# Two layers of a hybrid decoder: the norms of the rows one tile behind their sums, and three weight pieces split ahead of the last expert pair

## The chip, the cores and the metric

One core of a Trainium2 chip runs the whole program in one launch. The metric is the device time of one execution in microseconds (us), median of several; lower is better. The core's engines run side by side, each with its own queue of instructions that it works off in order: TensorE (PE) multiplies matrices, VectorE (DVE) and GpSimd (POOL) work elementwise, ScalarE (ACT) applies functions and copies, SyncE (SP) issues most DMAs. SBUF is the on-chip memory, PSUM holds what PE writes.

## What is computed

A decoder trunk of two layers over 512 tokens of width 1024. Each layer has a token mixer and a mixture of 32 experts, both behind a norm that is modulated by vectors computed from `c`; a last norm ends the program. Cut to what matters here:

```
for layer in range(2):
    h = rmsnorm(x, norm_mix_g) * (1 + sc_mix) + sh_mix
    x = x + g_mix * token_mixer(h, w_in, ..., w_out)      # begins with h @ w_in
    h = rmsnorm(x, norm_ffn_g) * (1 + sc_ffn) + sh_ffn
    x = x + g_ffn * moe(h, ...)                            # 4 groups x 8 experts, 2 per token
return rmsnorm(x, final_norm_g)                            # x * rsqrt(mean(x*x) + 1e-6) * g
# moe: y += (silu(t @ w_gate) * (t @ w_up) * weight of the token) @ w_down, per expert
```

## The kernel before

The tokens stand in four row tiles of 128 (i = 0 to 3). The 32 experts are worked off as 16 pairs, n = 0 to 15, one pair in a matmul of 128 rows. The loop over the pairs (L1816 to L1836) issues `gate_up(n)`, then `down(n-1)`, so that a pair's silu on ACT and DVE (L770 to L774, tiles `sg`, `sge`) runs beside other matmuls. `down(n)` transposes the pair's hidden rows on PE (L1754), copies them to SBUF on ACT (`hT`, L1756), multiplies by w_down (L1767) and scales by the gate vector on DVE (`y`, L1773).

The rows of the first 12 pairs go through memory. Those of pairs 12 to 15 are put to their tokens by matmuls: ACT and POOL (or DVE) divide `y` into a rounded part `yh` (L1776) and its remainder `yl` (L1777), and `combine(n)` multiplies both by a 0/1 matrix (L1806, L1807) and adds the sum to `x` on DVE (L1808), eight times for a pair. For pair 15, `combine` goes tile by tile, and behind each half of a tile it sums its squares on ACT (`junk`, L1446); in layer 0, POOL besides scales the half for the next norm (tile `z`, L1450).

After that stand the norms. `route_norm(i)` adds the two half sums on DVE (`ssum`, L1597) and calls `rstd`: DVE `m` (L569), ACT logarithm and exponential (L570, L571), DVE `nt` and `y` (L574, L578), all of one element per row. In layer 0, `next_hT` then makes the next mixer's input for each tile: DVE `z` (L662), eight PE transposes (L672) with copies into `hhi` (ACT) and `hlo` (DVE, L676). In the last layer, `final` writes each tile into a new tile `fy` (L1913) and sends it (L1914); the gain `fg` is loaded on ACT's queue (L1909).

A weight piece of the mixer is likewise used as a rounded part and its remainder. A piece is 512 rows by up to 512 columns, loaded to a tile `w` and split in two halves by `split`: ACT writes the rounded part (L240), then `lo_engine`, which is DVE unless it is set, the remainder (L241). `splitter` returns the function `get` that makes splits when they are first asked for; `in_open` makes that function for a layer's pieces of `w_in`, and `next_hT` asks for the first halves between the tiles. Their matmuls are L740 (hi by hi), L741 and L742.

The loads of all weights go out on SP in one order (L216), each when a slot of SBUF is free; `rows`, the next norm's vectors spread over all partitions, is loaded by two DMAs on ACT's queue (L531), which `next_open` issues in the code behind `down(15)`.

The order on each engine is set by a scheduler from the order of the code; where `pin` or `keep_in_program_order` is set, the instruction keeps its place in the code's order.

Of the kernel before, what the change touches and what calls it, by code (L numbers as in the profile page):

```python
# [10 lines left out]
F32 = mybir.dt.float32  # L11
# [124 lines left out]
class Kernel:  # L136
# [366 lines left out]
    def ada_fin(self, l, v):  # L503
        V, T, acc, c = self.V, self.T, self.acc, self.c
        if (l, v) == (0, 0):
            vec = self.const([P, 2, NK], F32, "vec")
            p = self.pb()
            rows = self.ident.rearrange("p (v j r) -> p j v r", v=2, j=2)[:, :, :, 0]
            for j in range(2):
                for k in range(NK):  # L510
                    T.matmul(p[j * 64:j * 64 + 64, 2 * k:2 * k + 2], acc.rearrange("p (q k) -> p k q", k=NK)[:, k, :],
                             rows[:, j], start=True, stop=True)
            part = self.split
            self.split = lambda w, n, los=[V, V, self.G]: self.pinned(part, los.pop(0), w, n)
            self.in_open(0)
            self.split = part
            V.tensor_tensor(vec, p[:, 0:2 * NK].rearrange("p (k v) -> p v k", v=2),
                            c["bada"].rearrange("p (v k) -> p v k", v=2), op=OP.add)
            V.scalar_tensor_tensor(vec[:, 1], vec[:, 1], 1.0, c["gmix"], op0=OP.add, op1=OP.mult)
            self.vec[(0, 0)], self.vec[(0, 1)] = vec[:, 0], vec[:, 1]  # L520
            return
# [80 lines left out]
            self.next_hT(l)  # L602

    def in_open(self, l):
        self.hhi = [self.u([P, 4, L], F32R, "hhi") for _ in range(2)]
        self.hlo = [self.u([P, 4, L], F32R, "hlo") for _ in range(2)]
        self.get = self.splitter([st for st in self.mseq[l] if st[0] == "in"] + self.oseq[l])
        if l == 0:
            self.get(("in", l, 0, 0), 0)

    def first_hT(self):
        V, S, G, T = self.V, self.S, self.G, self.T
# [39 lines left out]

    def next_hT(self, l):
        V, S, G, T = self.V, self.S, self.G, self.T
        self.mixer_slots()
        self.in_open(l)
        self.mixer_open(l)
        for i in range(NT):
            self.route_norm(i)
            h = self.h[i]  # L660
            self.tc.keep_in_program_order(
                V.scalar_tensor_tensor(h, h, self.r[i], self.rows[:, 0], op0=OP.mult, op1=OP.add))  # L662
            if i < 3:
                self.pin = True
                self.get(("in", l, 0, 0), 0, i + 1)
                self.pin = False
            self.nc.scalar.dma_start(self.xd[i * P:(i + 1) * P, :], self.xt[i])
            hh = h.rearrange("p (q k) -> p q k", k=NK)
            for g in range(2):
# [944 lines left out]
    def moe(self, l):  # L1614
# [184 lines left out]
        def combine(n):  # L1799
            for a in range(8):  # L1800
# [8 lines left out]
                if n == NE // 2 - 1:  # L1809
                    self.route_half(i, half)  # L1810
                    if half and self.h:
                        self.route_scale(i, half)

        self.reserve, got = 3, None
        self.pump()
        for n in range(NE // 2):  # L1816
            gate_up(n)
            if n == 0:
                self.overflow(l, *over)
# [18 lines left out]
            self.next_open(l + 1)  # L1838
        else:
            self.h, self.ssq, self.r = {}, {}, {}  # L1840
        combine(NE // 2 - 1)

    def overflow(self, l, cnti, ov):
# [17 lines left out]
        with self.tc.If(any_ > 0):  # L1861
            nc.scalar.dma_start(self.ovd, ov.rearrange("p i e -> p (i e)"))
            nc.scalar.dma_start(self.ovc, cnti[:, 0:NE])
            with self.tc.For_i(0, NE, 1) as e:
                nc.scalar.dma_start(ce, self.ovc[:, ds(e, 1)])
                here = nc.values_load(ce[0:1, 0:1], min_val=0, max_val=2 * L)
                with self.tc.If(here > 0):
# [7 lines left out]
                    for i in range(NT):  # L1875
# [21 lines left out]
                        for h in range(2):  # L1897
                            cs = slice(h * 512, h * 512 + 512)
                            p = pd
                            for f in range(2):  # L1900
# [2 lines left out]
                            V.scalar_tensor_tensor(self.xt[i][:, cs], y, wv[:, i:i + 1], self.xt[i][:, cs],  # L1903
                                                   op0=OP.mult, op1=OP.add)

    def final(self):
        V, S = self.V, self.S
        g = self.t4([P, D], F32, "fg")
        self.nc.scalar.dma_start(g, self.dap("final_norm_g", 0, [[0, P], [1, D]]))  # L1909
        for i in range(NT):  # L1910
            self.route_norm(i)
            y = self.t4([P, D], F32, "fy")
            V.scalar_tensor_tensor(y, self.xt[i], self.r[i], g, op0=OP.mult, op1=OP.mult)  # L1913
            self.nc.sync.dma_start(bass.AP(tensor=self.out.tensor, offset=self.out.offset + i * P * D,  # L1914
                                           ap=[[D, P], [1, D]]), y)


    def merge(self, main, sides):
# [69 lines left out]
```

## Time and profile before

| | |
|---|---|
| median of 3 runs | 1335.87 us (1334.55 to 1336.6) |
| profiled execution | 1337.54 us |
| its span (first to last instruction) | 1335.8 us |
| mean granted TensorE clock | 0.95 of full speed |
| PE, DVE, ACT, POOL busy | 87%, 54%, 30%, 26% of the span |
| second layer's first matmul of `w_in` starts | 694.22 us |
| first final row starts | 1325.57 us |

All times in the rows below are microseconds from the span's start in the one profiled execution. A timeline row reads: start, duration, engine (with a q where a DMA is issued), line, operation, what is written from what, shape, count; in brackets the idle time of that engine before it and what ended it. A row with a count above 1 covers several instructions in succession, and its duration is from the first's start to the last's end.

### The profile page before, as it was taken

Reading aid. Unit: us, or ns where it says so; the run is one execution under the profiler, and the core shown is the slowest. Engines: PE = TensorE matmul, PEld = TensorE weight load, DVE = VectorE, ACT = ScalarE, POOL = GpSimd, SP = SyncE. Lnnn points to the kernel's source line nnn. Section 1 sums busy time; section 2 is a strip of 40 time slices with the busy share of each in tenths; the row PEclk is TensorE's granted clock in tenths of the full one; section 3 lists DMA queues with packets and bytes.
Section 4 is the critical chain, followed back from the end, with each engine's and each line's share of the span. In section 5 each row is a group of like instructions: output and inputs, shape, how many; then the busy total and the mean of one; then the engine's idle time right before and its main releaser. Section 6 shows DMA issues by size and latency. Waiting matters only on the chain. (4 is left out here: it accounts for less than half of the span.)

```text
span 1335.8 us, 16642 instructions
## 1 busy us (share of the span) xinstructions
PE 1164.3 (87%) x5900; PEld 729.9 (55%) x5902; DVE 718.7 (54%) x1576; ACT 401.1 (30%) x1029; POOL 350.7 (26%) x299
## 2 busy tenths in 40 slices
PE   4888899999999988788969998999898999888785
PEld 3666566666774443345347765767576644334432
DVE  3786877876671211123686576787777221112266
ACT  3442422545321211111135332345352121111113
POOL 0252323461242111111033222346133321111100
PEclk9898989999989999997989997989999999999898
DMA  9973256462877999999972221463276899999972
GB/s 377 400 283 116 76 190 248 124 228 63 312 239 281 413 411 403 391 397 403 392 265 77 73 95 36 171 228 116 94 285 209 261 409 412 413 411 411 401 315 79
DMA packets 104861, 350.95 MB, mean 263 GB/s; under 512 B 16875, under 2 KB 27883, under 8 KB 90435
## 3 DMA queue, kind: packets, MB, share of 16 engines
q1 hardware_dynamic: 85936, 313.31, 61.7%
q10 hardware_dynamic: 10738, 22.24, 4.8%
q0 software_dynamic: 8096, 14.24, 3.0%
q8 instruction: 51, 0.84, 0.3%
q14 instruction: 40, 0.32, 0.1%
HBM read 333.35 MB, written 29.48 MB: 272 GB/s over the span
## 5 line engine op out<-in xcount | busy, mean ns | idle before, releaser
L1732 PE MATMUL pa<-w,X 128*64 128x512 f32 x1024 | 259.0, 605 | 41.9 <-DMA w<-w_up 35.2
L1732 PEld LDWEIGHTS pa<-w,X 128*64 128x64 f32 x1024 | 102.7, 138 | 163.5 <-issue 113.9
L1767 PE MATMUL pb<-w,hT 128*64 128x512 f32 x512 | 137.9, 639 | 11.8 <-ACT hT L1756 10.7
L740 PE MATMUL pa<-wp,hhi 128*128 128x512 f32 x320 | 135.1, 426 | 3.7 <-ACT hhi L639 3.6
L741 PE MATMUL pa<-wp,hhi 128*128 128x512 f32 x320 | 130.1, 407 | 0.9 <-DVE wp L241 0.9
L742 PE MATMUL pa<-wp,hlo 128*128 128x512 f32 x320 | 128.3, 403 | 0.8 <-DVE hlo L640 0.8
L1741 DVE TENSOR_SCALAR sg<-pa 128x256 f32<-128x256 f32 x32 | 13.6, 424 | 208.4 <-PE pa L1732 208.4
L241 DVE TENSOR_TENSOR wp<-w,wp 128x1024 fp32r<-128x1024 f32 (+1 forms) x71 | 93.7, 1328 | 38.0 <-ACT wp L240 37.7
L1780 POOL DMA_INDIRECT yd<-y,idx x24 | 24.0, 1001 | 306.9 <-DVE y L1770 265.3
L240 ACT ACTIVATE wp<-w 128x1024 fp32r<-128x1024 f32 (+1 forms) x72 | 72.3, 1014 | 94.6 <-PE pa L742 38.3
L1767 PEld LDWEIGHTS pb<-w,hT 128*64 128x64 f32 x512 | 47.8, 145 | 78.1 <-issue 46.4
L1717 ACT ACTIVATE X<-pa 128x512 f32<-128x512 f32 x56 | 31.9, 598 | 183.1 <-PE pa L1716 164.5
L740 PEld LDWEIGHTS pa<-wp,hhi 128*128 128x128 f32 x320 | 62.1, 195 | 27.8 <-issue 6.5
L1770 DVE TENSOR_TENSOR y<-pb,gbc 128x512 f32<-128x512 f32 x48 | 33.2, 692 | 73.3 <-PE pb L1767 72.5
L770 ACT ACTIVATE sge<-sg 128x256 f32<-128x256 f32 x32 | 13.2, 412 | 197.8 <-DVE sg L1741 184.0
L742 PEld LDWEIGHTS pa<-wp,hlo 128*128 128x128 f32 x320 | 62.2, 195 | 16.8 <-issue 1.7
L741 PEld LDWEIGHTS pa<-wp,hhi 128*128 128x128 f32 x320 | 62.7, 196 | 15.2 <-DVE wp L241 1.9
L919 POOL TENSOR_TENSOR QX<-E,qk 128x1024 f32<-128x1024 f32 x16 | 40.6, 2536 | 96.6 <-ACT E L917 58.8
L1337 PE MATMUL pa<-wp,mhi 128*128 128x512 f32 x128 | 52.7, 411 | 0.7 <-ACT mhi L1310 0.5
L1339 PE MATMUL pa<-wp,mlo 128*128 128x512 f32 x128 | 51.8, 404 | 1.2 <-DVE mlo L1311 1.2
L935 PE MATMUL pb<-QX,E 64*128 64x128 f32 x448 | 43.8, 293 | 9.4 <-DVE hkg L1012 5.3
L1338 PE MATMUL pa<-wp,mhi 128*128 128x512 f32 x128 | 50.9, 398 | 0.0
(350 smaller groups left out, 2184.7 us busy)
## 6 DMA issues: line engine op xcount, KB each, us to landing
w<-w_gate SPq DMA_DIRECT2D x128, 512.0 KB
w<-w_up SPq DMA_DIRECT2D x128, 512.0 KB
w<-w_down SPq DMA_DIRECT2D x64, 1024.0 KB
w<-w_ada SPq DMA_DIRECT2D x48, 1024.0 KB
w<-w_in SPq DMA_DIRECT2D x16, 1024.0 KB
w<-w_in SPq DMA_DIRECT2D x16, 512.0 KB
yd<-Sblk SPq DMA_DIRECT2D x8, 1024.0 KB
w<-w_out SPq DMA_DIRECT2D x8, 1024.0 KB
```

Of the source, the lines that this page charges most:

```text
L240: keep(self.S.activation(hi, w[:, sl, :], AF.Copy))
L241: keep(self.lo_engine.tensor_tensor(lo, w[:, sl, :], hi.bitcast(F32), op=OP.subtract))
L740: T.matmul(acc[i], hh[:, s], wh, start=k == 0, stop=False)
L741: T.matmul(acc[i], hh[:, s], wl, start=False, stop=False)
L742: T.matmul(acc[i], hl[:, s], wh, start=False, stop=k == NK - 1)
L919: G.tensor_tensor(qx, e, qk[i][:, pr, None, :].to_broadcast([P, 8, P]), op=OP.mult)
L935: T.matmul(o, e[r, lv, :], qx[r, lv, :], start=True, stop=True)
L1337: T.matmul(acc, mh[kh][:, kk, s], hi[:, kk % 2, :], start=first, stop=False)
L1338: T.matmul(acc, mh[kh][:, kk, s], lo[:, kk % 2, :], start=False, stop=False)
L1339: T.matmul(acc, ml[kh][:, kk, s], hi[:, kk % 2, :], start=False, stop=last)
L1732: mm = T.matmul(p[j * 64:j * 64 + 64, :], X[h][:, kh * 4 + kk, ep * P + j * 64:ep * P + j * 64 + 64], w[j][:, :, kk], start=kh == 0 and kk ...
L1767: T.matmul(p[j * 64:j * 64 + 64, :], hT[:, f, j * 64:j * 64 + 64], w[j][:, f, cs], start=f == 0, stop=f == 1)
```

## The change

Three edits.

1. `in_open(l)` no longer makes `hhi` and `hlo` (a new `hh_open` does) and always asks for its first pieces. For layer 1 it is called ahead of `gate_up(15)` of layer 0, with `pin` set and POOL as the engine of the remainder. That is three splits: both halves of the first piece of `w_in` and the first half of the second. `next_hT` no longer asks for splits between the tiles. For layer 0 the order is as before.
2. In `combine(15)`, `route_norm(i - 1)` stands behind the second half of tile i, for i = 1 to 3. The last tile's norm stays where it was.
3. In the last layer, the final row of tile i - 1 is formed there too, in place in `x`, without the tile `fy`; `final_open` issues the load of `fg`.

```
 def in_open(self, l):
-    self.hhi = [self.u([P, 4, L], F32R, "hhi") for _ in range(2)]
-    self.hlo = [self.u([P, 4, L], F32R, "hlo") for _ in range(2)]
     self.get = self.splitter([st for st in self.mseq[l] if st[0] == "in"] + self.oseq[l])
-    if l == 0:
-        self.get(("in", l, 0, 0), 0)
+    self.get(("in", l, 0, 0), 0)
+
+def hh_open(self):
+    self.hhi = [self.u([P, 4, L], F32R, "hhi") for _ in range(2)]
+    self.hlo = [self.u([P, 4, L], F32R, "hlo") for _ in range(2)]
...
 def next_hT(self, l):
-    self.mixer_slots()
-    self.in_open(l)
+    self.hh_open()
     self.mixer_open(l)
     for i in range(NT):
-        self.route_norm(i)
+        if i not in self.r:
+            self.route_norm(i)
...
-        if i < 3:
-            self.pin = True
-            self.get(("in", l, 0, 0), 0, i + 1)
-            self.pin = False
...
 def combine(n):
...
                     if half and self.h:
                         self.route_scale(i, half)
+                    if half and i > 0:
+                        self.route_norm(i - 1)
+                        if not self.h:
+                            self.final_tile(i - 1)
...
         for n in range(NE // 2):
+            if n == NE // 2 - 1 and l + 1 < DEPTH:
+                self.mixer_slots()
+                self.pin, self.lo_engine = True, G
+                self.in_open(l + 1)
+                self.pin, self.lo_engine = False, V
             gate_up(n)
...
             self.h, self.ssq, self.r = {}, {}, {}
+            self.final_open()
         combine(NE // 2 - 1)
...
+def final_open(self):
+    self.fg = self.t4([P, D], F32, "fg")
+    self.nc.scalar.dma_start(self.fg, self.dap("final_norm_g", 0, [[0, P], [1, D]]))
+
+def final_tile(self, i):
+    x = self.xt[i]
+    self.V.scalar_tensor_tensor(x, x, self.r[i], self.fg, op0=OP.mult, op1=OP.mult)
+    self.nc.sync.dma_start(bass.AP(tensor=self.out.tensor, offset=self.out.offset + i * P * D,
+                                   ap=[[D, P], [1, D]]), x)
+
 def final(self):
-    V, S = self.V, self.S
-    g = self.t4([P, D], F32, "fg")
-    self.nc.scalar.dma_start(g, self.dap("final_norm_g", 0, [[0, P], [1, D]]))
-    for i in range(NT):
-        self.route_norm(i)
-        y = self.t4([P, D], F32, "fy")
-        V.scalar_tensor_tensor(y, self.xt[i], self.r[i], g, op0=OP.mult, op1=OP.mult)
-        self.nc.sync.dma_start(bass.AP(tensor=self.out.tensor, offset=self.out.offset + i * P * D,
-                                       ap=[[D, P], [1, D]]), y)
+    self.route_norm(NT - 1)
+    self.final_tile(NT - 1)
```

What this does to the order on the engines, at three places. In the names, the first number counts the tiles and the last one the writes; `w_985` and `w_986` are the first two pieces of the next layer's `w_in`.

ACT at the last pair of layer 0, before. The two `yh` at the top belong to pair 13, `sge` to the silu of pair 15, `hT` and the last two `yh` to pair 14.

```order
L1776 ACTIVATE yh_963_4952<-y_966_4959 128x512
L1776 ACTIVATE yh_963_4952<-y_968_4968 128x512
L770 ACTIVATE sge_986_5053<-sg_985_5051 128x256
L1756 ACTIVATE hT_988_5062<-pb_987_5059 128x256
L773 ACTIVATE sge_986_5053<-sge_986_5053 128x256
L531 DMA rows_1015_5151<-vecd_115 128x1024
L774 ACTIVATE sge_986_5053<-sge_986_5053 128x256
L531 DMA rows_1015_5151<-vecd_115 128x1024
L1776 ACTIVATE yh_989_5064<-y_992_5071 128x512
```

The same place on ACT now.

```order
L1774 ACTIVATE yh_963_4952<-y_966_4959 128x512
L1774 ACTIVATE yh_963_4952<-y_968_4968 128x512
L240 ACTIVATE wp_979_5024<-w_985_5033 128x1024
L240 ACTIVATE wp_980_5025<-w_985_5033 128x1024
L240 ACTIVATE wp_981_5026<-w_986_5039 128x1024
L532 DMA rows_1015_5153<-vecd_115 128x1024 x2
L768 ACTIVATE sge_989_5062<-sg_988_5060 128x256
L1754 ACTIVATE hT_991_5071<-pb_990_5068 128x256
L771 ACTIVATE sge_989_5062<-sge_989_5062 128x256
L772 ACTIVATE sge_989_5062<-sge_989_5062 128x256
L1774 ACTIVATE yh_992_5073<-y_995_5080 128x512
```

Three splits and both DMAs of `rows` now stand ahead of the silu of pair 15 and of the `hT` for which PE's `down(14)` waits. In the program, the first of the two DMAs waits for POOL's remainder of `wp_980`, since `rows_1015` is given the place of `w_985` in SBUF, and POOL's remainder is the last that reads it.

DVE at the start of the norms behind the last pair of layer 0, before. The two rows ahead are the last sums into `x`; `z_1016` is the next mixer's input of tiles 0 and 1.

```order
L1808 TENSOR_TENSOR x_518_2749<-pb_1033_5201,x_518_2749 128x512
L1808 TENSOR_TENSOR x_518_2749<-pb_1036_5209,x_518_2749 128x512
L1597 TENSOR_TENSOR ssum_1050_5231<-ssq_1019_5160 128x1
L569 TENSOR_SCALAR m_1051_5233<-ssum_1050_5231 128x1
L574 SCALAR_TENSOR_TENSOR nt_1053_5238<-m_1051_5233,y_1052_5234 128x1
L1597 TENSOR_TENSOR ssum_1056_5259<-ssq_1024_5175 128x1
L578 SCALAR_TENSOR_TENSOR y_1052_5234<-nt_1053_5238,y_1052_5234 128x1
L569 TENSOR_SCALAR m_1057_5261<-ssum_1056_5259 128x1
L662 SCALAR_TENSOR_TENSOR z_1016_5154<-z_1016_5154,y_1052_5234,rows_1015_5151 128x1024
L241 TENSOR_TENSOR wp_1038_5216<-w_983_5047,wp_1038_5216 128x1024
```

The same place on DVE now, from the last sum into `x`; the first `ssum` and `m` stand among the sums.

```order
L1806 TENSOR_TENSOR x_518_2749<-pb_1044_5231,x_518_2749 128x512
L575 SCALAR_TENSOR_TENSOR nt_1031_5195<-m_1029_5190,y_1030_5191 128x1
L579 SCALAR_TENSOR_TENSOR y_1030_5191<-nt_1031_5195,y_1030_5191 128x1
L1595 TENSOR_TENSOR ssum_1037_5213<-ssq_1024_5177 128x1
L570 TENSOR_SCALAR m_1038_5215<-ssum_1037_5213 128x1
L575 SCALAR_TENSOR_TENSOR nt_1040_5220<-m_1038_5215,y_1039_5216 128x1
L1595 TENSOR_TENSOR ssum_1046_5238<-ssq_1033_5202 128x1
L579 SCALAR_TENSOR_TENSOR y_1039_5216<-nt_1040_5220,y_1039_5216 128x1
L570 TENSOR_SCALAR m_1047_5240<-ssum_1046_5238 128x1
L575 SCALAR_TENSOR_TENSOR nt_1049_5245<-m_1047_5240,y_1048_5241 128x1
L579 SCALAR_TENSOR_TENSOR y_1048_5241<-nt_1049_5245,y_1048_5241 128x1
L664 SCALAR_TENSOR_TENSOR z_1016_5156<-z_1016_5156,y_1030_5191,rows_1015_5153 128x1024
```

Between the last sum and the first `z` there stood six small instructions: the norm of tile 0 with `ssum` and `m` of tile 1. Now the rest of the norms of tiles 0 to 2 stands there, with the `ssum` of tile 3, and no remainder of a weight piece follows.

DVE at the end of the last layer, before.

```order
L1808 TENSOR_TENSOR x_1484_7670<-pb_1993_10104,x_1484_7670 128x512
L1597 TENSOR_TENSOR ssum_1996_10112<-ssq_1976_10062 128x1
L569 TENSOR_SCALAR m_1997_10114<-ssum_1996_10112 128x1
L574 SCALAR_TENSOR_TENSOR nt_1999_10119<-m_1997_10114,y_1998_10115 128x1
L1597 TENSOR_TENSOR ssum_2001_10125<-ssq_1981_10075 128x1
L578 SCALAR_TENSOR_TENSOR y_1998_10115<-nt_1999_10119,y_1998_10115 128x1
L569 TENSOR_SCALAR m_2002_10127<-ssum_2001_10125 128x1
L1913 SCALAR_TENSOR_TENSOR fy_2000_10122<-x_1483_7669,y_1998_10115,fg_1995_10110 128x1024
```

And now.

```order
L1595 TENSOR_TENSOR ssum_1986_10086<-ssq_1977_10064 128x1
L1806 TENSOR_TENSOR x_1484_7670<-pb_1993_10105,x_1484_7670 128x512
L570 TENSOR_SCALAR m_1987_10088<-ssum_1986_10086 128x1
L1806 TENSOR_TENSOR x_1484_7670<-pb_1999_10123,x_1484_7670 128x512
L575 SCALAR_TENSOR_TENSOR nt_1989_10093<-m_1987_10088,y_1988_10089 128x1
L1595 TENSOR_TENSOR ssum_1995_10111<-ssq_1982_10077 128x1
L1806 TENSOR_TENSOR x_1484_7670<-pb_2002_10130,x_1484_7670 128x512
L579 SCALAR_TENSOR_TENSOR y_1988_10089<-nt_1989_10093,y_1988_10089 128x1
L570 TENSOR_SCALAR m_1996_10113<-ssum_1995_10111 128x1
L1920 SCALAR_TENSOR_TENSOR x_1483_7669<-x_1483_7669,y_1988_10089,fg_1975_10058 128x1024
```

The first tile's norm stands among the last sums into `x`, and ACT's logarithm for it now stands between the sums of squares and not behind all of them; the first final row follows two small instructions behind the last sum.

## Rows read from the trace of the kernel before

**Rows 1.** The page's first part: busy time of each engine, its share of the span, and its instructions.

```profile
PE 1164.3 (87%) x5900; PEld 729.9 (55%) x5902; DVE 718.7 (54%) x1576; ACT 401.1 (30%) x1029; POOL 350.7 (26%) x299
```

**Rows 2.** The waits of PE over the whole span. Columns: engine, tile and line that waited, for what; total us, times, longest us.

```profile
PE pb L672 <- DVE z L662: 9.4, 2, 8.5
```

**Rows 3.** The timeline of ACT from 655 to 668 us, around the silu of pair 15.

```profile
660.14 0.42 ACT L770 ACTIVATE sge<-sg 128x256 f32<-128x256 f32 x1 [11.47 <-DVE sg L1741]
660.46 0.36 ACT L1756 ACTIVATE hT<-pb 128x256 f32<-128x256 f32 x1
...
664.71 0.33 ACTq L531 DMA_DIRECT2D rows<-vecd  x1
665.16 1.15 ACT L1776 ACTIVATE yh<-y 128x512 fp32r<-128x512 f32 x2 [3.53 <-DMA w<-w_in]
```

**Rows 4.** The timeline of PE from 655 to 672 us: the last transposes ahead of `down(14)`, `down(14)`, and the first matmuls of `combine(14)`.

```profile
659.49 0.50 PE L1754 MATMUL pb<-first,sg 128*128 128x128 f32 x2
660.88 3.65 PE L1767 MATMUL pb<-w,hT 128*64 128x512 f32 x16 [0.89 <-ACT hT L1756]
665.84 0.97 PE L1806 MATMUL pb<-yh,PT 128*128 128x512 f32 x3 [1.30 <-ACT yh L1776]
667.27 0.97 PE L1807 MATMUL pb<-yl,PT 128*128 128x512 f32 x3 [0.46 <-POOL yl L1777]
```

**Rows 5.** The DMA issues of SP in three stretches (640 to 646.5, 646.5 to 650, and 664 to 667 us): pieces of the next layer's `w_in`. A duration is the time that SP stands at the issue.

```profile
645.62 0.38 SPq L216 DMA_DIRECT2D w<-w_in  x1
...
646.89 9.28 SPq L216 DMA_DIRECT2D w<-w_in  x2
...
663.08 1.54 SPq L216 DMA_DIRECT2D w<-w_in  x1
```

**Rows 6.** Busy time of each engine in four stretches. Columns: window, us, busy us of PE, PEld, DVE, ACT and POOL with their instructions, granted clock of PE, DMA share, GB/s.

```profile
654.00:657.00 3.00, 3.00 (x16) 1.06 (x16) 2.70 (x3) 0.00 (x0) 0.00 (x0) 1.00 1.04 394
685.00:686.00 1.00, 0.00 (x0) 0.00 (x0) 1.00 (x2) 0.55 (x1) 1.00 (x2) 0.97 0.73 303
696.00:697.00 1.00, 1.00 (x5) 0.79 (x4) 1.00 (x2) 0.82 (x1) 0.00 (x0) 0.91 1.07 416
1318.00:1322.00 4.00, 3.28 (x13) 1.91 (x11) 4.00 (x8) 2.42 (x7) 0.00 (x0) 1.00 0.01 3
```

**Rows 7.** Prices of a split: all of ACT's rounded parts as a group (busy us, mean ns, idle before), and the one remainder that POOL makes in this kernel, at its start (timeline of POOL, 0 to 40 us).

```profile
L240 ACT ACTIVATE wp<-w 128x1024 fp32r<-128x1024 f32 x64 | 66.9, 1055 | 84.3 <-PE pa L742 38.3 <-DMA w<-w_in 16.3 <-PE pa L727 12.4
...
37.03 2.60 POOL L241 TENSOR_TENSOR wp<-w,wp 128x1024 fp32r<-128x1024 f32 x1 [36.57 <-ACT wp L240]
```

**Rows 8.** The timeline of all engines from 662 to 675 us: `y`, `yh` and `yl` of pairs 14 and 15.

```profile
662.87 0.69 DVE L1773 TENSOR_TENSOR y<-pb,gbc 128x512 f32<-128x512 f32 x1 [1.79 <-PE pb L1767]
...
665.93 1.29 POOL L1777 TENSOR_TENSOR yl<-y,yh 128x512 fp32r<-128x512 f32 x1 [17.66 <-ACT yh L1776]
...
673.91 0.69 DVE L1773 TENSOR_TENSOR y<-pb,gbc 128x512 f32<-128x512 f32 x1 [1.22 <-PE pb L1767]
...
674.64 0.63 ACT L1776 ACTIVATE yh<-y 128x512 fp32r<-128x512 f32 x1 [2.76 <-DVE y L1773]
```

**Rows 9.** The timeline of DVE from 677 to 692 us: the last sums into `x` of layer 0 and the norms.

```profile
677.26 0.69 DVE L1808 TENSOR_TENSOR x<-pb,x 128x512 f32<-128x512 f32 x1 [0.94 <-PE pb L1807]
...
678.47 4.36 DVE L1808 TENSOR_TENSOR x<-pb,x 128x512 f32<-128x512 f32 x7
682.75 0.69 DVE L1597 TENSOR_TENSOR ssum<-ssq 128x1 f32<-128x1 f32 x1
...
684.64 1.24 DVE L574 SCALAR_TENSOR_TENSOR nt<-m,y 128x1 f32<-128x1 f32 x1 [1.01 <-ACT y L571]
685.80 1.30 DVE L1597 TENSOR_TENSOR ssum<-ssq 128x1 f32<-128x1 f32 x1
687.02 1.30 DVE L578 SCALAR_TENSOR_TENSOR y<-nt,y 128x1 f32<-128x1 f32 x1
...
688.40 1.28 DVE L662 SCALAR_TENSOR_TENSOR z<-z,y,rows 128x1024 f32<-128x1024 f32 x1
689.61 1.22 DVE L241 TENSOR_TENSOR wp<-w,wp 128x1024 fp32r<-128x1024 f32 x1
690.74 0.21 DVE L574 SCALAR_TENSOR_TENSOR nt<-m,y 128x1 f32<-128x1 f32 x1
```

**Rows 10.** The timelines of POOL from 676 to 692 us and of PE from 680 to 700 us, the same stretch.

```profile
678.03 10.27 POOL L1450 TENSOR_TENSOR z<-x,rows 128x512 f32<-128x512 f32 x8 [1.36 <-DVE x L1808]
...
680.83 0.40 PE L1807 MATMUL pb<-yl,PT 128*128 128x512 f32 x1
689.75 1.97 PE L672 MATMUL pb<-first,z 128*128 128x128 f32 x8 [8.52 <-DVE z L662]
...
694.22 0.78 PE L740 MATMUL pa<-wp,hhi 128*128 128x512 f32 x1
```

**Rows 11.** The timelines of DVE and of ACT from 1317 to 1334 us, the end of the program, and of ACT's DMA issues from 1314 to 1317 us.

```profile
1318.90 4.36 DVE L1808 TENSOR_TENSOR x<-pb,x 128x512 f32<-128x512 f32 x7
...
1325.57 1.28 DVE L1913 SCALAR_TENSOR_TENSOR fy<-x,y,fg 128x1024 f32<-128x1024 f32 x1
...
1324.61 0.19 ACT L570 ACTIVATE y<-m 128x1 f32<-128x1 f32 x1
...
1315.15 0.35 ACTq L1909 DMA_DIRECT2D fg<-final_norm_g  x1
```

More of the change, by code (lines that the diff above doesn't have):

```diff
@@ L604, in in_open @@
     def in_open(self, l):
+        self.get = self.splitter([st for st in self.mseq[l] if st[0] == "in"] + self.oseq[l])
+        self.get(("in", l, 0, 0), 0)
+    def hh_open(self):
         self.hhi = [self.u([P, 4, L], F32R, "hhi") for _ in range(2)]
         self.hlo = [self.u([P, 4, L], F32R, "hlo") for _ in range(2)]
-        self.get = self.splitter([st for st in self.mseq[l] if st[0] == "in"] + self.oseq[l])
-        if l == 0:
-            self.get(("in", l, 0, 0), 0)
     def first_hT(self):
@@ L654, in next_hT @@
         V, S, G, T = self.V, self.S, self.G, self.T
-        self.mixer_slots()
-        self.in_open(l)
+        self.hh_open()
         self.mixer_open(l)
         for i in range(NT):
-            self.route_norm(i)
+            if i not in self.r:
+                self.route_norm(i)
             h = self.h[i]
```

## The prediction

> **What bounds the kernel now.** I read the busy shares first: PE works 87% of the span and no other engine over 54% [rows 1], so a change elsewhere counts only where PE stands still, or after its last matmul. PE's waits as a whole then show where the norms at the layer's boundary cost something: PE waits 9.4 us for `z`, 8.5 of them at once [rows 2]. The timelines of that place tell what is late. The first sum of pair 15 into `x` starts at 677.26 (call this X) and the first `z` at 688.40, which is X + 11.14 [rows 9]; PE, idle since 681.23, goes on at 689.75 and begins the next layer's first matmul at 694.22 [rows 10]. At the end of the program the first final row starts at 1325.57, after ACT's first logarithm at 1324.61 [rows 11]. The change works on both places. What it puts ahead of them, three splits, lands in a third: ACT is idle 11.47 us before it starts the silu of pair 15 at 660.14 [rows 3], which looks like free room. Whether it is depends on when the first pieces of `w_in` are there.
>
> **Part 1, the early splits: ACT's queue.** ACT's splits now stand ahead of the silu and of `hT`, which PE's `down(14)` waits for, and ahead of the two DMAs of `rows`. The first split waits for the load of the first piece. SP issues that load at 645.62 and the next ones up to 656.2 [rows 5], while the DMA engines are full at 394 GB/s [rows 6]. In the trace of before, ACT is released at 664.71 and 665.16 by a landing of `w_in` [rows 3]; by the program this is the second piece. A piece is 512 x 512 x 4 bytes = 1.05 MB, 2.7 us at 394 GB/s, so I estimate the first one at 662.0. It can't be later than 663.08, since an issue of SP that waits for it goes out then [rows 5].
>
> From there, step by step. First split on ACT, mean 1.06 us [rows 7]: 663.1. POOL's two remainders of that piece, each 2.60 us by the one that the kernel makes [rows 7]: 668.3. ACT's own second and third split are done by 665.8 and hide behind POOL. The first DMA of `rows` waits for POOL's second remainder, and ACT stands at it; two issues of 0.33 us [rows 3]: 669.0. Then `sge` to `hT` takes 0.32 [rows 3], `hT` to the first matmul of `down(14)` 0.42 (660.46 to 660.88) [rows 3, 4]: 669.8 and not 660.88, or +8.9.
>
> Part of this comes back. Before, `yh` was held up until 665.16 by ACT's stand at the second `rows`; that wait now lies ahead. From the first matmul to `y` 1.99 us (660.88 to 662.87), `y` to `yh` 0.73, `yh` to POOL's `yl` 0.77, and `yl` to the first matmul with it 1.34 [rows 4, 8]: 4.83, so 674.6 and not 667.27, or +7.3 at full clock. POOL's third remainder ends at about 670.9, before `yl` asks for POOL at about 673.3, and costs nothing. PE now is idle from 659.99 to 669.8, 9.8 us [rows 4]. The trace shows what an idle PE pays: idle from 681.23 for 8.52 us, its granted clock falls to 0.97 in the stretch 685 to 686, its first matmul of `w_in` takes 0.78, and the clock is back only in the stretch 696 to 697 [rows 6, 10]. By this, the first half of `down(14)` (the 1.99 us to `y`) runs at the lower of the two levels, 1.2 GHz for 2.4, and takes up to twice as long: +1.7. **Sum of part 1: +9.0.** Ends: 5.4 (first piece there 1.9 us earlier, clock up) to 10.1 (first piece at 663.08). Nearest to the rows is the middle value, as the landing is derived from two of them.
>
> The loads behind: in the program SP's next pieces now stand behind copies that wait for pair 15's `yl`. The three pieces that are in SBUF by then are 144 matmuls, at PE's mean of 1164.3 / 5900 = 0.2 us some 28 us of cover, against 2.7 us for a load. I put it at nothing; without the cover it is the rival below.
>
> **Part 2, the norms beside POOL.** What is moved is small: `ssum`, `m`, `nt`, `y`, one element per row. But `ssum`, `nt` and `y` took 0.69, 1.24, 1.30 and 1.30 us while POOL made its eight `z` (678.03 to 688.30), and `nt` took 0.21 once POOL was done [rows 9, 10]. So such an instruction is held as long as a POOL instruction, 10.27 / 8 = 1.28 us. Before, four of them stood ahead of the first `z`. Now ten do: the norms of tiles 0 to 2 and the `ssum` of tile 3. The first `ssum` stands among the sums (+0.7), the last sum ends at about X + 6.4, POOL at about X + 11.0 to 11.5, and between them some four of the remaining nine are held at 1.3 each; the last five, at about 0.2, follow POOL's end: first `z` at about X + 12.6, so **+1.5**. Not held, the limit would be ACT: in the last layer its sums of squares end at 1324.61, which is 6.9 behind the first sum (1318.90 - 1.21) [rows 9, 11]; three norms at about 0.45 and the last `nt` and `y` put the first `z` at X + 9.1, or -2.0. These are the ends, -2.0 to +1.5; the held rows are four against none, so I take the upper one.
>
> The Trainium skill, page "SBUF — State Buffer", section "Who interferes with whom", says that a VectorE instruction with two SBUF inputs contends with a GpSimd instruction that reads SBUF, and that one with at most one such input doesn't. It speaks against this part of the change: by it the sum has +1.5 here, without such a lock -2.0, and the rows of this case agree with it (1.24 to 1.30 us beside POOL, 0.21 after).
>
> **Part 3, behind the first `z`.** Three remainders on DVE go (one is seen at 689.61, 1.22 us, between the first two `z` [rows 9]), and PE starts matmuls after the first tile's transposes. But the `z` of tile 3 now takes the place of that remainder, 1.28 for 1.22. Before, the first matmul of `w_in` came 4.47 us after the first transposes, 0.9 of it PE's second wait for `z` [rows 2, 10]. I take 0.6 of this 0.9: **-0.6**, ends -2.5 (two remainders) and 0.
>
> **Part 4, the last layer.** No POOL instruction runs there. The first final row waited for a logarithm that stood behind all sums of squares. Now it waits for the last sum into `x`, 1318.90 + 4.36 = 1323.26 [rows 11], four small instructions among the sums and two behind, about 0.7 together: 1323.95 for 1325.57, **-1.6** (ends -1.2 and -1.8). The later rows follow at the same pace on DVE in both. The gain was issued at 1315.15, and in 1318 to 1322 the DMA engines are idle (share 0.01) [rows 6, 11], so it costs nothing that the load is written elsewhere. Writing in place of `fy` costs nothing either, nothing reads the old `x`.
>
> **Sum.** 9.0 + 1.5 - 0.6 - 1.6 = +8.3 on the profiled execution's 1337.54: 1345.8. That execution lies 1.7 above the median of 1335.87, so on the median 1344.2.
>
> **The rivals.** (a) *The cover holds*, the other side: the splits end inside ACT's 11.47 us of idle time. This decides at a first landing by 660.14 - 0.66 - 5.2 - 1.06 = 653.2. Then part 1 turns into a gain, as `yh` no longer waits for `rows`: 660.88 + 4.83 = 665.7 for 667.27, or -1.6, and with the other parts -2.3: 1333.6; with small instructions that aren't held (-2.0) 1330.1. For it speaks that SP issued the first piece at 645.62, 7.6 us before; against it the landings seen at 664.7 and the full queues. (b) *The early norms pay, and the clock stays up*: part 1 at +7.3, part 2 at -2.0, part 3 at -2.5, part 4 at -1.6, together +1.2: 1337.1. For it speaks that the order puts less behind POOL's end; against it the four held rows. (c) *Late pieces*: the loads that stand behind the copies come too late by three of them, 3 x 2.7 = 8 us on top: 1352. Against it the 28 us of cover. (d) That the change doesn't do what it says is out for the order, which shows the splits ahead of the silu.
>
> **How the numbers follow.** Forecast 0.76 (1344, its own range 1338.5 to 1347), (a) 0.10, (b) 0.10, (c) 0.04. A measurement of this kernel tells some 0.2% from no change, 2.7 us: faster is below 1333.2, slower above 1338.5. Of (a) half is faster, half the same; of (b) 0.07 the same, 0.03 slower; the forecast is slower in all its range. Faster 0.05, same 0.12, slower 0.83. The range of 1337 to 1347 holds the forecast and (b); (a) and (c) and the corners of the forecast's ends, under 0.2, stay outside.
>
> **What would show it.** Right: in the timeline of ACT, the three splits stand behind the landing at about 662, with an idle time of some 13 us before them, `sge` of pair 15 starts at about 669 and is preceded by POOL's remainder; PE waits 9 to 10 us ahead of `down(14)`; `nt`, `ssum` and `y` in the boundary take about 1.3 us beside POOL's `z`; the first final row comes 1.6 us sooner behind the last sum. Wrong: `sge` within 1 us of its old time (then (a)), remainders on POOL well below 2.6, small instructions of 0.2 us beside POOL (then (b)), or a PE wait for `wp` in the first pieces of `w_in` (then (c)).

## The result and the profile after

The changed kernel takes 1344.8 us, median of five runs (1342.11 to 1346.32); five runs of the kernel before, taken with it, have a median of 1334.55 (1332.63 to 1336.6). The ratio is 1.0057 with a 95% interval of 1.0033 to 1.0081, so it is 4 to 11 us slower; the two medians by themselves are 10.3 us apart, which lies inside that. The execution that was profiled took 1344.8 us, its span 1343.0; PE's granted clock was 0.948 on average.

The list of PE's waits shows two places: ahead of `down(14)` (L1765 now) PE waits 9.4 us for `hT`, where it waited 0.89 [rows 4], and ahead of the boundary's transposes 10.3 us, where it waited 8.5 [rows 2].

```profile
PE pb L1765 <- ACT hT L1754: 19.3, 14, 9.4
...
PE pb L670 <- DVE m L570: 10.3, 1, 10.3
```

(The second row names DVE's `m`, but the transposes need `z`: it ends at 700.50 + 1.28 = 701.78, and PE goes on at 701.84.)

The timeline of ACT shows the first, and answers to [rows 3].

```profile
663.47 2.00 ACT L240 ACTIVATE wp<-w 128x1024 fp32r<-128x1024 f32 x2 [13.34 <-DMA w<-w_in]
665.94 1.06 ACT L240 ACTIVATE wp<-w 128x1024 fp32r<-128x1024 f32 x1 [0.46 <-DMA w<-w_in]
669.29 0.81 ACTq L532 DMA_DIRECT2D rows<-vecd  x2
670.15 0.42 ACT L768 ACTIVATE sge<-sg 128x256 f32<-128x256 f32 x1 [3.16 <-DMA mc<-mix]
670.47 0.36 ACT L1754 ACTIVATE hT<-pb 128x256 f32<-128x256 f32 x1
```

ACT stands 13.34 us for the first piece, makes its splits, then stands at the two DMAs of `rows` until 669.29, and only then comes to `sge`, which had waited since the end of `sg`. What it stood for is on POOL: the three remainders end at 664.61 + 6.96 = 671.57, 2.32 us each, and the second of them at 669.25. (The row of `sge` names a DMA of `mc` as the end of the wait. That is a matter of which event came last in the list: in the run with the splits alone, below, the same wait at the same place is put down to POOL's `wp`, and where the DMAs of `rows` stand elsewhere, `sge` doesn't wait behind the splits.)

```profile
664.61 6.96 POOL L241 TENSOR_TENSOR wp<-w,wp 128x1024 fp32r<-128x1024 f32 x3 [14.86 <-ACT wp L240]
...
688.38 10.29 POOL L1448 TENSOR_TENSOR z<-x,rows 128x512 f32<-128x512 f32 x8 [1.35 <-DVE x L1806]
```

On PE [rows 4, 10], the transposes of pair 14 begin 1.5 us later than before, since the executions drift by such amounts well ahead of the change. From there on it is the chain: `down(14)` 9.9 us behind them and not 1.4, and it takes 4.97 us instead of 3.65.

```profile
660.96 0.50 PE L1752 MATMUL pb<-first,sg 128*128 128x128 f32 x2
670.89 4.97 PE L1765 MATMUL pb<-w,hT 128*64 128x512 f32 x16 [9.43 <-ACT hT L1754]
...
677.02 0.74 PE L1805 MATMUL pb<-yl,PT 128*128 128x512 f32 x2 [0.49 <-POOL yl L1775]
...
701.84 1.97 PE L670 MATMUL pb<-first,z 128*128 128x128 f32 x8 [10.27 <-DVE m L570]
703.64 0.79 PE L738 MATMUL pa<-wp,hhi 128*128 128x512 f32 x1
```

The windows of these stretches give the reason for the longer matmuls. While PE is idle its granted clock stands at 0.50 (1.2 GHz, the lower of its two levels), and it is at full speed (2.4 GHz) again after 674; columns are as in [rows 6].

```profile
664.00:668.00 4.00, 0.00 (x0) 0.00 (x0) 0.00 (x0) 2.53 (x3) 3.40 (x2) 0.50 0.91 355
673.00:674.00 1.00, 1.00 (x6) 0.20 (x4) 0.00 (x0) 0.00 (x0) 0.00 (x0) 0.71 0.84 344
674.00:675.00 1.00, 1.00 (x8) 0.40 (x6) 0.69 (x1) 0.08 (x1) 0.00 (x0) 1.00 0.07 29
```

On DVE [rows 9], the sums of pair 14 and the norms of the boundary:

```profile
677.56 1.29 DVE L1806 TENSOR_TENSOR x<-pb,x 128x512 f32<-128x512 f32 x2 [0.86 <-PE pb L1805]
678.77 0.68 DVE L1775 TENSOR_TENSOR yl<-y,yh 128x512 fp32r<-128x512 f32 x1
...
687.61 0.69 DVE L1806 TENSOR_TENSOR x<-pb,x 128x512 f32<-128x512 f32 x1 [0.91 <-PE pb L1805]
...
691.30 1.27 DVE L1595 TENSOR_TENSOR ssum<-ssq 128x1 f32<-128x1 f32 x1
...
694.35 0.67 DVE L575 SCALAR_TENSOR_TENSOR nt<-m,y 128x1 f32<-128x1 f32 x1
695.06 1.19 DVE L579 SCALAR_TENSOR_TENSOR y<-nt,y 128x1 f32<-128x1 f32 x1
696.17 1.29 DVE L1595 TENSOR_TENSOR ssum<-ssq 128x1 f32<-128x1 f32 x1
...
698.30 0.38 DVE L575 SCALAR_TENSOR_TENSOR nt<-m,y 128x1 f32<-128x1 f32 x1 [0.65 <-ACT y L572]
698.61 0.15 DVE L1595 TENSOR_TENSOR ssum<-ssq 128x1 f32<-128x1 f32 x1
...
699.85 0.22 DVE L575 SCALAR_TENSOR_TENSOR nt<-m,y 128x1 f32<-128x1 f32 x1 [0.91 <-ACT y L572]
...
700.50 1.28 DVE L664 SCALAR_TENSOR_TENSOR z<-z,y,rows 128x1024 f32<-128x1024 f32 x1 [0.21 <-issue]
```

Beside POOL's eight `z` (688.38 to 698.67), `ssum` takes 1.27 and 1.29, `y` 1.19 and `nt` 0.67 and 0.38; the `ssum` that starts at 698.61 takes 0.15. Two of the `nt` besides wait for ACT's logarithm and exponential, 0.65 and 0.91 us. The first `z` comes 700.50 - 687.61 = 12.89 us behind the first sum of pair 15; it was 11.14. The end of the program [rows 11] gains:

```profile
1326.76 0.69 DVE L1806 TENSOR_TENSOR x<-pb,x 128x512 f32<-128x512 f32 x1 [0.94 <-PE pb L1805]
...
1331.97 0.68 DVE L1806 TENSOR_TENSOR x<-pb,x 128x512 f32<-128x512 f32 x1
...
1332.75 1.28 DVE L1920 SCALAR_TENSOR_TENSOR x<-x,y,fg 128x1024 f32<-128x1024 f32 x1
```

The first final row starts 5.99 us behind the first sum of the last pair, where it started 7.88 behind it.

### The profile page after: what moved, and what is told of

Its sections match the earlier page's. It is cut to its first block, busy times and chain, and to the rows that moved or that the text cites. A ratio compares the mean times of both kernels' runs of the same rounds, so it can differ in the third digit from the quotient of the medians.

```text
span 1343.0 us, 16643 instructions
## 1 busy us (share of the span) xinstructions
PE 1163.2 (87%) x5900; PEld 731.2 (54%) x5902; DVE 714.1 (53%) x1573; ACT 402.0 (30%) x1029; POOL 359.0 (27%) x302
## 5 line engine op out<-in xcount | busy, mean ns | idle before, releaser
L1765 PE MATMUL pb<-w,hT 128*64 128x512 f32 x512 | 137.3, 629 | 19.8 <-ACT hT L1754 19.3
L738 PE MATMUL pa<-wp,hhi 128*128 128x512 f32 x320 | 137.2, 432 | 3.3 <-ACT hhi L641 3.2
L739 PE MATMUL pa<-wp,hhi 128*128 128x512 f32 x320 | 132.5, 415 | 0.8 <-DVE wp L241 0.8
L740 PE MATMUL pa<-wp,hlo 128*128 128x512 f32 x320 | 131.0, 411 | 0.8 <-DVE hlo L642 0.8
L241 DVE TENSOR_TENSOR wp<-w,wp 128x1024 fp32r<-128x1024 f32 (+1 forms) x68 | 89.9, 1331 | 37.2 <-ACT wp L240 36.6
L1765 PEld LDWEIGHTS pb<-w,hT 128*64 128x64 f32 x512 | 48.0, 143 | 85.2 <-issue 43.3
```

The costliest lines, as they stand in the source:

```text
L241: keep(self.lo_engine.tensor_tensor(lo, w[:, sl, :], hi.bitcast(F32), op=OP.subtract))
L738: T.matmul(acc[i], hh[:, s], wh, start=k == 0, stop=False)
L739: T.matmul(acc[i], hh[:, s], wl, start=False, stop=False)
L740: T.matmul(acc[i], hl[:, s], wh, start=False, stop=k == NK - 1)
L1765: T.matmul(p[j * 64:j * 64 + 64, :], hT[:, f, j * 64:j * 64 + 64], w[j][:, f, cs], start=f == 0, stop=f == 1)
```

## The experiments

Eight kernels ran, in two sets of four, each with its own runs of the kernel before. An execution of one kernel may differ from the next by several us (the kernel before ranged from 1328.75 to 1343.61 in 35 runs), so I read each experiment in its trace first, by five stretches that the change touches, and then hold the sum against the ratio. All stretches run from start to start: A, the transposes of pair 14 to the first matmul of `down(14)`; B, from there to X, the first sum of pair 15 into `x`; C, X to the first `z`; D, the first `z` to the 49th hi-by-hi matmul of the next `w_in`, where the first pieces are behind; E, the first sum of the last layer's pair 15 to its first final row.

| kernel | A | B | C | D | E | A to E against before | by the ratio |
|---|---|---|---|---|---|---|---|
| before | 1.39 | 16.38 | 11.14 | 48.13 | 7.88 | | |
| changed | 9.93 | 16.72 | 12.89 | 47.36 | 5.99 | +8.0 | +7.6 |
| splits alone | 10.10 | 17.58 | 11.16 | 47.96 | 7.82 | +9.7 | +9.6 |
| norms and rows alone | 1.39 | 19.12 | 12.66 | 47.12 | 5.99 | +1.4 | +0.3 |
| last layer alone | 1.39 | 15.60 | 11.14 | 48.44 | 6.00 | -2.4 | -2.3 |
| splits behind pair 14 | 1.39 | 17.24 | 12.77 | 46.84 | 6.00 | -0.7 | +0.7 |
| rows behind pair 14 | 6.22 | 16.84 | 12.81 | 47.44 | 5.99 | +4.4 | +2.7 |
| remainders on DVE | 7.97 | 17.14 | 12.67 | 46.65 | 6.00 | +5.5 | +6.4 |
| one-input norms | 1.39 | 16.07 | 9.21 | 47.91 | 6.15 | -4.2 | -2.7 |
| the same, rows early | 1.39 | 15.39 | 9.38 | 47.83 | 6.15 | -4.8 | -3.7 |

(Times in us; the last column is the ratio less 1, times 1336. Each row is one execution, and there is one trace of the kernel before. Every sum lies within the interval of its ratio.)

### The splits alone

```
 (changed kernel, combine)
-                    if half and i > 0:
-                        self.route_norm(i - 1)
-                        if not self.h:
-                            self.final_tile(i - 1)
...
 def final(self):
-    self.route_norm(NT - 1)
-    self.final_tile(NT - 1)
+    for i in range(NT):
+        self.route_norm(i)
+        self.final_tile(i)
```

> The change's early splits alone: the norms of layer 0's rows and the final rows stand where they stood before. Theory (ACT waits for the first piece's landing and for POOL's remainders): the first matmul of down(14) comes 8 to 10 us later relative to its transposes, the whole kernel 7 to 9 us slower than before (1.005 to 1.007). Rival (the norms beside POOL are the cost, the splits are covered): within 2 us of before, and PE's wait ahead of down(14) stays near 0.9 us.

Measured: ratio 1.0072 (1.0044 to 1.0100), A at 10.10.

```profile
660.80 0.50 PE L1752 MATMUL pb<-first,sg 128*128 128x128 f32 x2
670.90 6.60 PE L1765 MATMUL pb<-w,hT 128*64 128x512 f32 x16 [9.60 <-ACT hT L1754]
```

The splits make the loss; that the norms were its cause is out. In the traces they make more than the whole of it (9.7 for 8.0), which the times alone don't show, as the two intervals overlap.

### The norms and final rows alone

```
 for n in range(NE // 2):
-    if n == NE // 2 - 1 and l + 1 < DEPTH:
-        self.mixer_slots()
-        self.pin, self.lo_engine = True, G
-        self.in_open(l + 1)
-        self.pin, self.lo_engine = False, V
```

(and the splits between the tiles in `next_hT` as before.)

> The early norms and final rows alone, the splits where they stood before. Theory: the first z of the boundary 1.5 us later behind the first sum of pair 15 than the 11.1 us of before, the end of the program 1.7 us earlier, together within 1.5 us of before. Rival (norms are the cost): 5 us or more slower than before.

Measured: 1.0002 (0.9980 to 1.0024). C is 1.5 longer and E 1.9 shorter, as expected; the next stretch gives 1.0 of C back. What was not expected is B, 2.7 longer. The timeline of ACT shows most of it, 2.0 us: the second DMA of `rows` goes out only when a piece of `w_in` has landed, and `yh` stands behind it, 5.56 us here and 3.53 in the trace of before [rows 3].

```profile
667.02 0.33 ACTq L532 DMA_DIRECT2D rows<-vecd  x1
667.47 1.15 ACT L1781 ACTIVATE yh<-y 128x512 fp32r<-128x512 f32 x2 [5.56 <-DMA w<-w_in]
```

This isn't shown to be an effect of the norms. ACT has the same order here in four kernels, and the second DMA of `rows` goes out 5.2 us behind the transposes of pair 14 before, 7.2 here, and 4.4 and 4.9 in the runs of the last layer alone and of the one-input norms: B moves by such amounts with the landing. The rest, 0.7 us from the first matmul with `yl` to X, goes with the clock, which is at 0.50 behind PE's longer wait for `yh` (columns as in [rows 6]):

```profile
670.00:672.00 2.00, 2.00 (x6) 1.54 (x6) 1.66 (x4) 0.00 (x0) 0.00 (x0) 0.50 1.01 392
```

### The last layer alone

```
-                    if half and i > 0:
+                    if half and i > 0 and not self.h:
                         self.route_norm(i - 1)
```

(on top of the one before.)

> Early norms and rows in the last layer alone; layer 0 as before. Theory: first final row 6.0 to 6.3 us behind the first sum of pair 15 instead of 7.9, the kernel 1.5 to 1.8 us faster than before (about 0.9988), at the edge of what can be told. Rival (the write of the rows bounds the end, not the norms): no difference.

Measured: 0.9983 (0.9959 to 1.0007), which can't be told from no change by the times; in the trace E falls by 1.9, and the pitch of the four rows stays (5.0 and 4.9 us from first to last).

### The splits behind pair 14

```
 def split(self, w, n):
-    keep(self.S.activation(hi, w[:, sl, :], AF.Copy))
+    ins = keep(self.S.activation(hi, w[:, sl, :], AF.Copy))
+    if self.lo_engine is self.G and self.pin and hasattr(self, "last_yh"):
+        self.after(ins, self.last_yh)
...
             if n > 0:
                 down(n - 1, got)
+            if n == NE // 2 - 1 and l + 1 < DEPTH:
+                self.pin, self.lo_engine = True, G
+                self.next_open(l + 1)
+                self.mixer_slots()
+                self.in_open(l + 1)
+                self.pin, self.lo_engine = False, V
```

(`last_yh` is the last `yh` made, that of pair 14; the call ahead of `gate_up(15)` and the `next_open` behind `down(15)` are gone. The DMAs of `rows` move too, ahead of the silu.)

> The whole change, but the three splits stand behind the yh of pair 14 on ACT and the rows DMAs ahead of the silu of pair 15, in another place of SBUF; POOL still makes the remainders. Theory (the place on ACT's queue is the cost): PE's wait ahead of down(14) back to about 0.9 us, 8 to 11 us faster than the changed kernel, so 0 to 2 us faster than before. Rival (the later loads on SP or POOL's remainders cost): still 4 us or more slower than before.

Measured: 1.0005 (0.9986 to 1.0024), A back at 1.39: some 7 us faster than the changed kernel by the two ratios, where 8 to 11 were expected.

```profile
658.10 0.50 PE L1754 MATMUL pb<-first,sg 128*128 128x128 f32 x2
659.49 3.65 PE L1767 MATMUL pb<-w,hT 128*64 128x512 f32 x16 [0.89 <-ACT hT L1756]
```

The place on ACT's queue was the cost: the same three splits, with POOL's remainders, cost nothing in A from here. But B did not fall as it might have: `down(14)` to the first matmul with `yl` fell from 6.39 to 4.81, by the `rows` that now go out early, and then DVE's `yl` took 2.51 us beside a remainder on POOL, where it takes 0.68 alone. So here the splits cost some 1.8 us in B instead: from the first matmul with `yl` to X it is 12.43 us, and 10.58 in the last run below, which has the early `rows` and no splits here. The rows of DVE and POOL:

```profile
666.05 2.51 DVE L1777 TENSOR_TENSOR yl<-y,yh 128x512 fp32r<-128x512 f32 x1
...
665.65 7.49 POOL L243 TENSOR_TENSOR wp<-w,wp 128x1024 fp32r<-128x1024 f32 x3 [1.40 <-ACT wp L240]
```

### The rows behind pair 14, and the remainders on DVE

Both keep the splits where the change put them, and shorten the chain behind the landing. The first ties the DMAs of `rows` to the `yh` of pair 14:

```
 def row(self, dst, l, v):
-        self.nc.scalar.dma_start(dst, ...)
+        ins = self.nc.scalar.dma_start(dst, ...)
+        if l and v < 2:
+            self.after(ins, self.yh14)
```

(`yh14` is the last `yh` of pair 14.)

> The change, with the two rows DMAs tied behind the yh of pair 14 on ACT: ACT no longer stands for POOL's second remainder, but still for the second piece's landing. Theory (chain of landing, split, POOL's remainders, rows): PE's wait ahead of down(14) falls from 9.4 to about 6.5 us, the rest of the stall stays; some 2 to 3 us of the 9.9 come back. Rival (the landing alone makes the stall, POOL's remainders are hidden): the wait stays at 9 us or more.

The second changes the engine:

```
-                self.pin, self.lo_engine = True, G
+                self.pin, self.lo_engine = True, V
```

> The change, with VectorE making the three early remainders. Theory: 1.3 us for a remainder in place of 2.3 on POOL, so rows, silu and hT come 2 us earlier: PE's wait ahead of down(14) about 7.5 us in place of 9.4, the kernel 2 us faster than the changed one. Rival (POOL's time is hidden): the wait is unchanged.

Measured: 1.0020 (0.9998 to 1.0043) with A at 6.22, and 1.0048 (1.0025 to 1.0071) with A at 7.97; PE's longest wait ahead of `down(14)` is 5.7 and 7.5 us. In the first, `sge` follows the third split at once (rows of PE, then of ACT):

```profile
665.83 5.10 PE L1767 MATMUL pb<-w,hT 128*64 128x512 f32 x16 [5.72 <-ACT hT L1756]
...
664.15 1.06 ACT L240 ACTIVATE wp<-w 128x1024 fp32r<-128x1024 f32 x1 [0.46 <-DMA w<-w_in]
665.11 0.40 ACT L770 ACTIVATE sge<-sg 128x256 f32<-128x256 f32 x1
...
671.88 0.81 ACTq L532 DMA_DIRECT2D rows<-vecd  x2
```

In the second, DVE needs 1.24 us for a remainder, and the DMAs of `rows` still stand between the splits and `sge`; but they are out by 664.26 + 1.33 = 665.59, and what `sge` waits for last is DVE's `sg`, which now stands behind the three remainders and ends at 666.65 (rows of PE, of ACT, then of DVE):

```profile
667.43 5.97 PE L1765 MATMUL pb<-w,hT 128*64 128x512 f32 x16 [7.46 <-ACT hT L1754]
...
664.26 1.33 ACTq L532 DMA_DIRECT2D rows<-vecd  x2
666.68 0.42 ACT L768 ACTIVATE sge<-sg 128x256 f32<-128x256 f32 x1 [1.63 <-DMA mc<-mix]
...
662.59 3.72 DVE L241 TENSOR_TENSOR wp<-w,wp 128x1024 fp32r<-128x1024 f32 x3 [2.85 <-ACT wp L240]
666.23 0.42 DVE L1739 TENSOR_SCALAR sg<-pa 128x256 f32<-128x256 f32 x1
```

The wait of 7.5 us was the one expected, but in part by luck: the expectation had the chain through `rows`, and `sg` put about 1 us more on it, while the first piece landed earlier behind the transposes (2.0 us, 2.5 in the changed kernel).

From the changed kernel to the rows behind pair 14, A falls by 9.93 - 6.22 = 3.7 us, where 2 to 3 were expected; 0.45 of that is a landing that came 2.06 us behind the transposes and not 2.51. In the changed kernel's own trace the stand at `rows` (POOL's remainders and the two issues) is the 3.16 us of idle time ahead of `sge`, and the rest of 9.93 - 1.39 = 8.54, 5.4, is the landing and the splits themselves.

### One tensor from SBUF

```
 def rstd(self, ssq, n, shape):                               # where shape[1] == 1
-            V.scalar_tensor_tensor(t, m, y, y, op0=OP.mult, op1=OP.mult)
+            V.tensor_scalar(t, m, y, y, op0=OP.mult, op1=OP.mult)
...
-        V.scalar_tensor_tensor(y, t, 3.0, y, op0=OP.add, op1=OP.mult)
+            V.tensor_scalar(y, t, 3.0, y, op0=OP.add, op1=OP.mult)
...
 def route_norm(self, i):
-        self.V.tensor_tensor(s, self.ssq[i][:, 0:1], self.ssq[i][:, 1:2], op=OP.add)
+        self.V.tensor_scalar(s, self.ssq[i][:, 0:1], self.ssq[i][:, 1:2], None, op0=OP.add)
```

(on top of the norms and final rows alone.)

> Early norms and final rows, splits where they stood before, and ssum, nt and y written as tensor_scalar with a per-row scalar in place of the second tensor, so that each takes at most one tensor from SBUF. Theory (POOL holds up VectorE instructions with two SBUF inputs): these take 0.15 to 0.25 us beside POOL's z, the first z comes at X + 9 to 10 in place of X + 12.7, the kernel 2 to 4 us faster than with the early norms alone. Rival (any VectorE instruction beside POOL is slow, or ACT bounds the norms): they stay near 1.3 us, or the first z stays at X + 12.

Measured: 0.9980 (0.9957 to 1.0003). The times alone don't tell it from the early norms alone, whose interval overlaps; the trace does. Rows of DVE, then of POOL:

```profile
681.40 0.69 DVE L1816 TENSOR_TENSOR x<-pb,x 128x512 f32<-128x512 f32 x1 [0.94 <-PE pb L1815]
...
682.61 2.56 DVE L1816 TENSOR_TENSOR x<-pb,x 128x512 f32<-128x512 f32 x4
...
687.07 0.26 DVE L575 TENSOR_SCALAR nt<-m,y 128x1 f32<-128x1 f32 x1
687.37 0.21 DVE L580 TENSOR_SCALAR y<-nt,y 128x1 f32<-128x1 f32 x1
687.50 0.20 DVE L1605 TENSOR_SCALAR ssum<-ssq 128x1 f32<-128x1 f32 x1
...
690.61 1.71 DVE L670 SCALAR_TENSOR_TENSOR z<-z,y,rows 128x1024 f32<-128x1024 f32 x1
692.24 2.29 DVE L241 TENSOR_TENSOR wp<-w,wp 128x1024 fp32r<-128x1024 f32 x1
...
682.17 11.28 POOL L1458 TENSOR_TENSOR z<-x,rows 128x512 f32<-128x512 f32 x8 [1.36 <-DVE x L1816]
```

`nt`, `y` and `ssum` take 0.26, 0.21 and 0.20 us in the midst of POOL's `z`, where they took 0.67, 1.18 and 1.30 at the same place with the early norms alone, and the first `z` stands at X + 9.21 (X is the row at 681.40). The two that still read two tensors, `z` and the remainder of a piece, are held (1.71 and 2.29 for 1.28 and 1.22 [rows 9]), and POOL needs 11.28 for its eight `z` in place of 10.27. The rewriting changes the operation as well as the number of tensors, but the sums into `x` settle which of the two counts: they are `tensor_tensor` with one input from PSUM and one from SBUF, and four of them take 2.56 us beside POOL's `z` (the row at 682.61), as they do in the last layer, where POOL has none.

### The same, with the rows early

```
             if n > 0:
                 down(n - 1, got)
+            if n == NE // 2 - 1 and l + 1 < DEPTH:
+                self.next_open(l + 1)
```

> As the one before, and the two rows DMAs issued ahead of the silu of pair 15, in another place of SBUF; splits where they stood before. Theory: down(14) to the first matmul with yl falls from 6.4 to 4.8 us (seen with the splits behind pair 14), so 1.6 us on top; with the norms -1.5 to -3 and the end of the program -1.8, 4 to 6 us faster than before (0.995 to 0.997). Rival (what is won at the norms is lost again at the first weight pieces): within 2 us of before.

Measured: 0.9972 (0.9954 to 0.9991), median 1332.62 for 1336.35. It is faster than both kernels, 1 to 6 us faster than the one before; 4 to 6 were expected. That the early `rows` add to the one-input norms isn't shown by the times, whose intervals overlap. In the traces the first matmul with `yl` comes 4.81 us behind the first of `down(14)`, and 6.08 without them; 0.6 of that goes again before X, so B is 0.7 shorter. The timeline of ACT has both `rows` ahead of the silu, at 652.42, and `yh` now waits for nothing but `y`.

```profile
652.42 2.82 ACTq L532 DMA_DIRECT2D rows<-vecd  x2
658.42 0.42 ACT L778 ACTIVATE sge<-sg 128x256 f32<-128x256 f32 x1 [11.48 <-DVE sg L1749]
...
661.87 0.63 ACT L1784 ACTIVATE yh<-y 128x512 fp32r<-128x512 f32 x1 [2.01 <-DVE y L1781]
```

## Why the prediction held, step by step

**Part 1, the early splits.** Forecast +9.0 at the first matmul with `yl`, measured from the transposes 16.06 for 7.78, +8.3, and +8.9 at X. *The landing.* Estimated at 662.0, which is 2.5 us behind the transposes of pair 14; measured 663.47, 2.5 behind them. That it fits so well is luck in part: in the three other runs with the splits ahead of the silu the piece landed 2.0 to 2.7 behind. *POOL's remainders* were priced at 2.60 by the one row there was; they took 2.32, which is 0.6 for two, and more than the whole of what A came out shorter (8.5 for 8.9 forecast). *The clock*: +1.7 forecast, 4.97 - 3.65 = +1.3 measured, as the clock rose within the first half of `down(14)`. This too varies: `down(14)` takes 5.10, 5.97 and 6.60 us in the other runs with that stall, +1.5 to +3.0. *Not foreseen*: from the first matmul with `yl` to X 10.59 us and not 9.99. In the changed order DVE makes two sums ahead of its `yl` (the two rows at 677.56 and 678.77), for which PE's next matmul waits; the same 10.6 is in the runs with the rows behind, the remainders on DVE, and the rows early.

**Which link of the chain costs what** was argued in the prediction and is shown now: the place ahead of the silu (A back at 1.39 with the splits and `rows` moved), the stand at `rows` for POOL (3.2 of the 8.5), the landing and ACT's splits (5.4).

**The loads behind** were put at nothing, and D is not longer in the changed kernel (47.36 for 48.13), so this held, and rival (c) fell; no wait of PE above 0.2 us in D is for `wp`. What the splits give back where they were meant to is small too: with the splits alone, X to the 49th matmul (C and D) is 59.1 for 59.3.

**Part 2, the norms beside POOL.** +1.5 forecast, +1.75 measured in the changed kernel and +1.5 in the norms alone. That they are held is as forecast, the count is not: four instructions were to be held for 1.3 us behind the last sum, and the trace has two (1.19 and 1.29), two held for less (0.67 and 0.38), and two waits for ACT (0.65 and 0.91) that the forecast's sum didn't have. So the nearness of the two numbers is luck in part. The lower bound, -2.0 for instructions that aren't held, has also been measured: with one tensor from SBUF each, 9.21 - 11.14 = -1.9. The rule of the Trainium skill, page "SBUF — State Buffer", section "Who interferes with whom", which weighed in for the upper end, is borne out: 0.67 to 1.30 us with two inputs from SBUF and 0.20 to 0.27 with one, at the same place and beside the same POOL instructions.

**Part 3, behind the first `z`.** -0.6 forecast, D 47.36 for 48.13, -0.8. PE's second wait for `z` (0.88) is gone, of which the forecast took 0.6. The remainders that left DVE aren't needed for that: with the norms alone, which keep them, the wait is gone as well. The first matmul of `w_in` comes 3.1 us behind the first `z` and not 5.8, but that is PE's order and no gain, as from there to the 49th it takes 44.2 and not 42.3. **Part 4, the last layer.** -1.6 forecast, -1.9 measured, and -1.9 again in the last layer alone.

**The sum.** +8.3 forecast, +8.0 in the trace, +7.6 by the ratio. Rival (a), the cover, fell at its own point: it would have decided from a landing 6.3 us ahead of the transposes of pair 14 (653.2 for 659.49), and the first piece landed 2.5 us behind them. Rival (b) fell with the held rows. The median of 1344.8 against 1344.2 is closer than the method can claim, as the interval alone is 6 us wide; that is luck.

**Open.** Why the stretch from the next layer's `w_in` to its last pair differs by up to 6 us from one execution to the next (575.0 to 581.2 from the end of D to the start of E in the ten traces, though nothing was changed there) wasn't looked into. It is the reason why differences of 2 us are shown here by stretches of the traces, and not by times.

## What to carry to other kernels

Idle time ahead of an instruction is cover only for work whose data are there: look up when the transfer lands, and if that is behind the instruction that ends the idle time, the work belongs behind it, since an engine works off its queue in order. (Behind pair 14 the splits cost nothing in A, but by the times they gained nothing either.) A DMA issue on a compute engine's queue is such an instruction too: whatever it waits for (a slot of SBUF, an earlier load), the engine waits for, and here two of them, issued earlier, no longer held up `yh` (0.7 us of B in the traces, too little for the times to show). And before a chain of small VectorE instructions is put beside GpSimd's work, write them with one tensor from SBUF.

## What the runs showed of the hardware

- A per-row scalar operand that is read from SBUF does not make a `tensor_scalar` wait for POOL, even with two of them (`nt`, 0.26 us beside POOL); a second tensor from SBUF does, even one of a single element per row (`y` 1.19, `ssum` up to 1.30 us); one from PSUM doesn't (the sums into `x`). Undisturbed, the form with scalars is a little slower: in the last layer `nt` takes 0.26 to 0.27 us for 0.21, and the four final rows 5.25 from first to last, for 4.93 with the early norms alone.
- A held VectorE instruction goes through when the POOL instruction under way is done, not after POOL's whole queue: `ssum` takes at most 1.30 us beside `z` of 10.27 / 8 = 1.28, and the `yl` of 2.51, with the splits behind pair 14, ends 0.5 us behind POOL's first remainder (665.65 + 2.36 = 668.01). POOL pays in turn: the longest of its three remainders there takes 2.84 us, the shortest 2.36.
- PE's clock was at 0.50 after an idle stretch of 9.4 us and back at 1.00 some 3 us after PE went on (670.89 to 674), but only 6 us after in the run with the splits alone (670.90, and 1.00 from 677); after the boundary's idle time of 8.5 us in the trace of before it took until 696, 6 us after 689.75 [rows 6, 10].
